# Projection operands kept in DRAM between two token halves, the recurrent unit cut into jobs of its own, the embedding moved to the front

## The chip, the cores and the metric

The kernel runs on one core of one Trainium2 chip. The metric is device time in microseconds. A core has TensorE (PE, matmuls and weight loads), VectorE (DVE), ScalarE (ACT), GpSimd (POOL) and SyncE (SP), which here issues nearly all DMA.

## The reference

One decoder block over 2048 tokens of width 1024, all in float32. Cut to what matters:

```python
xn = rmsnorm(h, pre_gain)
q, k, v, fl, g_attn, x_lru, g_lru = split(xn @ w_in)
o_attn = forgetting_attention(q, k, v, fl + b_f)        # 8 heads of 128, causal, decay bias
y_attn = rmsnorm(o_attn, attn_out_gain) * silu(g_attn)
xc = causal_depthwise_conv(x_lru, conv_w, conv_b)       # width 4
r = sigmoid(xc @ w_r + b_r); i = sigmoid(xc @ w_i + b_i)    # 8 blocks of 128
log_a = -8 * r * softplus(-lam); a = exp(log_a)
u = sqrt(-expm1(2 * log_a)) * (i * xc)
o_lru[t] = a[t] * o_lru[t-1] + u[t]
y_lru = rmsnorm(o_lru, lru_out_gain) * silu(g_lru)
h = h + rmsnorm(concat(y_attn, y_lru) @ w_out, post_gain)
e = rmsnorm(p @ w_ple, ple_gain)
out = h + sigmoid(h @ w_ple_gate + b_ple_gate) * e
```

## The kernel before

Every float32 product is made of three fp32r matmuls (`mm3`): each operand is split into a rounded high part and the remainder (`split`: ACT writes the high part, DVE or POOL the low part).

The input projection is cut into units of two output blocks. A unit multiplies a 2 x 2 arrangement of weight quarters and input quarters in the Strassen-Winograd form: seven products instead of eight. The seven input operands `XH`/`XL` are made once per half of the tokens (1024 of them, p = 0 and 1) by `fill_operand`; the seven weight operands are made for each unit by `Unit.prepare`: sums and differences of the raw quarters `wf` on POOL (`ws`), then the split into `oh` and `ol`, five of each deep (`NOP`). `operand` prepares as far ahead as those buffers allow. Units are of four kinds: v (values and forget logits, the weights moving, 258 columns), k (keys and queries of one head), l (the recurrent input x_lru and its gate g_lru of one block) and g (the attention gate). A k, l or g unit issues 7 x 12 matmuls of 512 columns, a v unit 7 x 4 x 12 of 258 columns. `multiply` issues one product of the seven, `pair` adds the products up; the sum `t5 = t2 + t5` is POOL's, as the split for i = 2 is.

The units run in this order: v 0 of the first half, twenty mixed l, k and g units, v 1 of the first half, v 0 of the second half, sixteen l and k units, v 1, and four g units, marked `light`, for which DVE does what POOL does elsewhere. Two k units are marked `early`: products 0 and 5 of each come before v 0, as soon as the first inputs are there.

An l unit carries the recurrent unit with it (`lru_unit`), on 1024 columns: convolution, gate matmuls (12 of 512 columns), sigmoid, tanh, `Dn = 1/(1 + tanh)` by RECIPROCAL on DVE, square root, scan over time with a carried state, times the gate `G`, store to `yl_d`, and the squares summed in `accl`. Its second part, `gates`, waits in `pending` and is run inside the next unit. Row sums of x for the first norm come from a separate load of x by rows (`row_scales`).

Then comes attention with an order written out by hand, and in the third part the recurrent half of the output mixing with, for each of 16 token blocks, `embed`: 12 matmuls of 512 columns for p @ w_ple, its norm, and a store to `e_d`. The last part mixes the attention half, adds the residual and applies the embedding gate.

Outside the attention part the order on each engine is set by a scheduler that works through the program by priority of program order and its own estimate of times, so an engine's instructions need not stand as the code is written.

## Time and profile before

| what | value |
|---|---|
| three runs, median (lowest to highest) | 2380.26 us (2377.54 to 2383.28) |
| the profiled execution | 2383.02 us |
| its span, first to last instruction | 2381.2 us |
| PE / DVE / POOL / ACT busy share | 92% / 68% / 49% / 44% |
| DMA moved | 276.32 MB |
| granted TensorE clock, mean | 0.969 |

The span is what the trace covers; the run is 1.8 us longer. Shares are means over stages with different limits, so the stages have to be read one by one.

### The profile page before, as it was taken

What the parts mean: (1) busy time and instruction counts of PE and PEld (TensorE: products, weight loads), DVE (VectorE), ACT (ScalarE), POOL (GpSimd) and SP (SyncE); (2) the same over time, 40 slices, a digit from 0 to 9 for tenths busy, and PEclk for the clock granted to TensorE, in tenths of its full rate; (3) what the DMA queues carried; (4) which work ended last, traced back from release to release, by engine and by line L of the source; (5) the groups of instructions that cost most, each with busy time, mean ns of one, the idle gap of its engine ahead of it and who ended that gap; (6) DMA issues with size and microseconds to landing.
All of it is one profiled execution on the core that took longest, in us unless ns stands there. A gap on an engine that the chain in (4) does not pass through costs nothing. (4 is left out here: it accounts for less than half of the span.)

```text
span 2381.2 us, 30652 instructions
## 1 busy us (share of the span) xinstructions
PE 2200.0 (92%) x10753; PEld 1807.6 (76%) x10753; DVE 1612.8 (68%) x2363; ACT 1039.8 (44%) x1786; POOL 1172.8 (49%) x865
## 2 busy tenths in 40 slices
PE   4798899998898999889989999999999999999999
PEld 4676677767786777668768888888878888788887
DVE  5886978788967888887767888887853313333333
ACT  4344444444333433452447676766753423212211
POOL 5766767677666766765312333433453322322221
PEclk9799999999999999999989999999999999999999
DMA  6224232223322222223345444545435535433332
GB/s 217 74 62 126 80 120 82 83 75 110 124 86 74 85 77 69 78 70 101 114 157 133 130 131 139 161 150 144 149 113 164 193 128 186 133 115 111 111 103 83
DMA packets 180922, 276.32 MB, mean 116 GB/s; under 512 B 15392, under 2 KB 84256, under 8 KB 180768
## 3 DMA queue, kind: packets, MB, share of 16 engines
q1 hardware_dynamic: 180624, 274.33, 37.2%
q8 instruction: 84, 1.38, 0.2%
q14 instruction: 70, 0.57, 0.1%
q10 hardware_dynamic: 144, 0.05, 0.0%
HBM read 198.55 MB, written 75.76 MB: 115 GB/s over the span
## 5 line engine op out<-in xcount | busy, mean ns | idle before, releaser
L64 PE MATMUL bank<-XH,oh 128*128 128x512 f32 x1120 | 454.5, 406 | 35.4 <-ACT oh L50 22.4
L66 PE MATMUL bank<-XH,ol 128*128 128x512 f32 x1120 | 450.5, 407 | 35.4 <-DVE ol L56 24.4
L65 PE MATMUL bank<-XL,oh 128*128 128x512 f32 x1120 | 451.0, 403 | 0.0
L66 PEld LDWEIGHTS bank<-XH,ol 128*128 128x128 f32 x1120 | 216.8, 194 | 98.6 <-DVE ol L56 31.8
L64 PEld LDWEIGHTS bank<-XH,oh 128*128 128x128 f32 x1120 | 217.2, 194 | 94.8 <-ACT oh L50 30.4
L65 PEld LDWEIGHTS bank<-XL,oh 128*128 128x128 f32 x1120 | 217.1, 194 | 50.5
L56 DVE TENSOR_TENSOR tl<-tbank,th 128x512 fp32r<-128x512 f32 (+1 forms) x320 | 192.7, 608 | 86.5 <-ACT th L50 82.7
L50 ACT ACTIVATE th<-tbank 128x512 fp32r<-128x512 f32 (+1 forms) x320 | 168.8, 530 | 130.5 <-PE tbank L845 127.4
L50 ACT ACTIVATE oh<-ws 128x512 fp32r<-128x512 f32 (+1 forms) x144 | 90.6, 629 | 267.6 <-POOL ws L215 130.9
L56 POOL TENSOR_TENSOR yo<-yf,yh 128x1024 fp32r<-128x1024 f32 x32 | 76.8, 2401 | 255.2 <-ACT yh L50 255.1
L56 POOL TENSOR_TENSOR ol<-wf,oh 128x512 fp32r<-128x512 f32 (+1 forms) x88 | 129.2, 1471 | 134.7 <-ACT oh L50 120.0
L278 DVE TENSOR_TENSOR c<-bank,c 128x512 f32<-128x512 f32 x208 | 137.9, 680 | 70.9 <-POOL c L292 35.3
L818 ACT ACTIVATE pr<-pr,m 128x128 f32<-128x128 f32 (+15 forms) x128 | 154.0, 1204 | 42.6 <-DVE m L809 41.8
L845 PE MATMUL tbank<-ident,pr 128*128 128x128 f32 x1088 | 172.4, 274 | 0.0
L50 ACT ACTIVATE oh<-wf 128x512 fp32r<-128x512 f32 (+1 forms) x192 | 117.0, 624 | 117.8 <-PE bank L65 57.3
L845 PEld LDWEIGHTS tbank<-ident,pr 128*128 128x128 f32 x1088 | 134.7, 141 | 29.4 <-issue 0.4
L64 PE MATMUL bank<-oh,XH 128*128 128x258 f32 x448 | 133.1, 302 | 24.8 <-ACT XH L50 11.9
L64 PE MATMUL sbank<-kh,qh 128*128 128x512 f32 (+3 forms) x320 | 137.5, 430 | 17.5 <-DVE m L809 17.5
L66 PE MATMUL bank<-oh,XL 128*128 128x258 f32 x448 | 129.7, 298 | 12.3 <-DVE XL L56 12.3
L65 PE MATMUL bank<-ol,XH 128*128 128x258 f32 x448 | 133.3, 300 | 5.7 <-DVE ol L56 3.9
L56 DVE TENSOR_TENSOR ol<-ws,oh 128x512 fp32r<-128x512 f32 (+1 forms) x100 | 101.4, 1015 | 35.0 <-ACT oh L50 34.7
L64 PE MATMUL obank<-th,vh 128*128 128x512 f32 (+1 forms) x320 | 123.5, 386 | 0.8 <-ACT th L50 0.8
(237 smaller groups left out, 5648.5 us busy)
## 6 DMA issues: line engine op xcount, KB each, us to landing
wf<-in_w_p_dram SPq DMA_DIRECT2D x164, 256.0 KB, 2.7
wf<-in_w_v_dram SPq DMA_DIRECT2D x32, 258.0 KB, 3.0
c<-in_x_dram SPq DMA_DIRECT2D x32, 256.0 KB, 4.6
s<-in_xT_dram SPq DMA_DIRECT2D x16, 512.0 KB, 7.8
kT_d<-c SPq DMA_DIRECT2D x32, 256.0 KB, 2.5
qT_d<-c SPq DMA_DIRECT2D x32, 256.0 KB, 2.8
...
yl_d<-G SPq DMA_DIRECT2D x16, 512.0 KB, 2.6
```

Of the source, the lines that this page charges most:

```text
L50: nc.scalar.activation(hi, src, AF.Copy)
L56: eng.tensor_tensor(out=lo, in0=src, in1=f32(hi), op=ALU.subtract)
L64: nc.tensor.matmul(out, lhsT=wh, rhs=xh, start=start, stop=False)
L65: nc.tensor.matmul(out, lhsT=wh, rhs=xl, start=False, stop=False)
L66: nc.tensor.matmul(out, lhsT=wl, rhs=xh, start=False, stop=stop)
L278: nc.vector.tensor_tensor(out=o, in0=x, in1=y, op=ALU.add)
L818: nc.scalar.activation(pr[0][:, :L], pr[0][:, :L], AF.Exp, bias=m2, scale=-1.0, accum_out=u.r4[:, i:i + 1])
L845: nc.tensor.transpose(b[:, i * P:(i + 1) * P], u.P[i][:, sb * P:(sb + 1) * P], ident)
```

## The change

Weight operands: in the first half of the tokens a unit makes each operand as before, in one tile `op` that holds high and low part, and stores it to DRAM (`wo_d`, `vo_d`); in the second half `fetch` loads it, and nothing is made or split. Nine operands can then be held: five `op` and four pairs `wh`, `wl` in the buffers of the raw quarters.

The recurrent unit: an l unit now only stores x_lru to `xr_d` and the gated value of g_lru to `gl_d`. A job (`lru_job`) of 512 columns loads them back, in two steps eight slots apart; a slot is one product (`tick`). Eight of the 32 jobs are planned into the first half, 24 into the second, five slots apart. Instead of the reciprocal a job computes, with `Dn` = 1 + exp(-2z) and two fused steps, one Newton step for 1/(1 + tanh z). R, I, Dn, Q and G have one buffer each.

The embedding is computed first of all, from a pool that is closed before three of the seven input operands are allocated. The column sums of x for the first half's norm come from the already loaded xT (`column_scales`). The two early k units and `light` are gone; the first half runs all l, then all k, then all g units; the second all l, all k, v 1, then g. `t5` and the split for i = 2 are DVE's everywhere.

```diff
+        def fetch(self, i):
+            n = WS if self.kind == "v" else 512
+            for hf in range(self.halves):
+                at_ = state["slot"] % (NOP + NOPB)
...
+                if at_ < NOP:
+                    op = wp.tile([P, 2, WS], F32R, name="op", bufs=NOP)
+                    nc.sync.dma_start(out=f32(op[:, :, :n]), in_=self.stored(i, hf))
+                else:
+                    hi = wp.tile([P, WS], F32R, name="wh", tag="wf", bufs=8)
+                    lo = wp.tile([P, WS], F32R, name="wl", tag="wf", bufs=8)
...
         def prepare(self, i):
+            if self.p:
+                return self.fetch(i)
...
-                split(nc, src, hi[:, :n], lo[:, :n], "act", "pool" if i in (0, 2, 5) and not self.light else "dve")
+                split(nc, src, hi[:, :n], lo[:, :n], "act", "pool" if i in (0, 5) else "dve")
+                nc.sync.dma_start(out=self.stored(i, hf), in_=f32(op[:, :, :n]))
...
-    mids = [("l", 0), ("k", 0), ("g", 0), ("l", 1), ("k", 1), ("l", 2), ("k", 2), ("g", 1), ("l", 3), ("k", 3),
+    mids_A = [("l", n) for n in range(8)] + [("k", n) for n in range(8)] + [("g", n) for n in range(4)]
+    mids_B = [("l", n) for n in range(8)] + [("k", n) for n in range(8)]
...
-        (nc.vector if u.light else nc.gpsimd).tensor_tensor(out=t5, in0=t2, in1=t5, op=ALU.add)
+        add(t5, t2, t5)
...
+    def lru_job(lw, accl, hb, c, t):
+        def first():
...
+            X = lw.tile([P, 515], F32, name="X", bufs=2)
+            nc.sync.dma_start(out=X, in_=xr_d[hb, :, c * 512:c * 512 + 515])
...
+        def second():
...
+                b = sbank()
+                mm3(nc, b, (j.w[0][:, gi], j.w[1][:, gi]), (j.xch, j.xcl), True, True)
+                nc.scalar.activation(dst, b, AF.Sigmoid, bias=vec[:, bias + hb:bias + hb + 1])
+            nc.scalar.activation(Dn, R, AF.Exp, scale=sp4n[:, hb:hb + 1])
             nc.scalar.activation(R, R, AF.Tanh, scale=sp4[:, hb:hb + 1])
-            nc.vector.tensor_scalar(Dn, R, 1.0, None, ALU.add)
-            nc.vector.reciprocal(Dn, Dn)
-            nc.scalar.activation(Q, R, AF.Sqrt, scale=4.0, bias=tiny)
+            nc.scalar.activation(Dn, Dn, AF.Identity, bias=one)
             nc.gpsimd.tensor_tensor(out=I, in0=I, in1=XC, op=ALU.mult)
+            nc.vector.scalar_tensor_tensor(out=Q, in0=R, scalar=1.0, in1=Dn, op0=ALU.add, op1=ALU.mult)
+            nc.vector.scalar_tensor_tensor(out=Dn, in0=Q, scalar=-4.0, in1=Dn, op0=ALU.add, op1=ALU.mult)
+            nc.scalar.activation(Q, R, AF.Sqrt, scale=0.25, bias=tiny)
+            nc.vector.tensor_tensor(out=R, in0=R, in1=Dn, op=ALU.mult)
             nc.vector.tensor_tensor(out=Q, in0=Q, in1=Dn, op=ALU.mult)
+            nc.scalar.activation(Dn, R, AF.Identity, scale=0.5, bias=one)
+            nc.gpsimd.tensor_tensor(out=I, in0=I, in1=Q, op=ALU.mult)
             nc.vector.tensor_tensor_scan(R, Dn, I, carry[:, hb:hb + 1] if c else 0.0, ALU.mult, ALU.add)
+            nc.gpsimd.tensor_tensor(out=G, in0=R, in1=G, op=ALU.mult)
+            nc.sync.dma_start(out=yl_d[hb, :, c * 512:(c + 1) * 512], in_=G)
+                nc.gpsimd.tensor_tensor(out=R, in0=R, in1=R, op=ALU.mult)
+                nc.gpsimd.tensor_tensor(out=acc, in0=acc, in1=R, op=ALU.add)
+        at_slot(t, first)
+        at_slot(t + JLAG, second)
...
+        embed_weights()
+        embeds(1)
         for n in range(2):
-            row_scales(sg, 0, n)
             for kh in range(2):
                 s[n, kh] = stage_tile(sg, 0, n, kh)
+        embeds(5)
+        for n in range(2):
+            column_scales(sg, 0, n, s)
             r = spread_scales(sg, 0, n)
...
+        plan_jobs(lw, accl, 60, 9.5, 8)
...
+        plan_jobs(lw, accl, 1, 5, 8)
+        plan_jobs(lw, accl, 46, 5, 16)
```

Below are three places of the built order. Line numbers are those of the kernel whose order is shown.

First, DVE at the start, before: from the spread norm factor `rx` on, the inputs `s` are scaled and the low parts `XL` of the first two input operands made.

```order
L483 COPY rx<-sbank 128x512
L489 SCALAR_TENSOR_TENSOR s_159<-s_159,vec,rx 128x512 x4
L489 SCALAR_TENSOR_TENSOR s_162<-s_162,vec,rx 128x512 x4
L56 TENSOR_TENSOR XL_109<-s_159,XH_102 128x512 x4
L56 TENSOR_TENSOR XL_114<-s_162,XH_107 128x512 x4
```

DVE at the same place now:

```order
L533 COPY rx<-sbank 128x512
L619 SCALAR_TENSOR_TENSOR eo<-bank,er,pgb 128x512 x2
L518 TENSOR_TENSOR rx<-rx,c 128x512
L539 SCALAR_TENSOR_TENSOR s_186<-s_186,vec,rx 128x512 x4
L539 SCALAR_TENSOR_TENSOR s_189<-s_189,vec,rx 128x512 x4
L619 SCALAR_TENSOR_TENSOR eo<-bank,er,pgb 128x512 x2
L518 TENSOR_TENSOR rx<-rx,c 128x512
L58 TENSOR_TENSOR XL_111<-s_186,XH_110 128x512 x2
L58 TENSOR_TENSOR pl<-pf,ph 128x512
L58 TENSOR_TENSOR XL_111<-s_186,XH_110 128x512 x2
L58 TENSOR_TENSOR XL_113<-s_189,XH_112 128x512 x4
```

The scaled embedding rows `eo`, their splits `pl` and the sums of column squares (`rx<-rx,c`) now stand between the steps that make the input operands; on PE all 192 embedding matmuls stand ahead of the first v unit.

Second, ACT in the second half of the tokens, before: the gates of one recurrent unit (`R`, `I`, tanh into `R`, square root into `X`) among the splits of weight operands (`oh`).

```order
L430 ACTIVATE R<-bank,vec 128x512
L50 ACTIVATE oh<-ws 128x512
L430 ACTIVATE R<-bank,vec 128x512
L430 ACTIVATE I<-bank,vec 128x512
L50 ACTIVATE wgh<-wgf 128x256
L430 ACTIVATE I<-bank,vec 128x512
L431 ACTIVATE R<-R,sp_90 128x1024
L435 ACT_TABLE_LOAD
L435 ACTIVATE X<-R,tiny 128x1024
L50 ACTIVATE oh<-ws 128x512
```

ACT in the second half now, about one job:

```order
L461 ACTIVATE I<-sbank,vec 128x512
L323 ACTIVATE c<-bank 128x512
L440 ACTIVATE XC<-X,vec 128x512
L461 ACTIVATE R<-sbank,vec 128x512
L462 ACT_TABLE_LOAD
L462 ACTIVATE Dn<-R,sp4n 128x512
L52 ACTIVATE xch<-XC 128x512
L463 ACTIVATE R<-R,sp_94 128x512
L464 ACTIVATE Dn<-Dn,one 128x512
L468 ACT_TABLE_LOAD
L468 ACTIVATE Q<-R,tiny 128x512
L414 ACT_TABLE_LOAD
```

The operand splits are gone, the jobs follow each other closely with three table loads each, and the copies that empty PE's banks (`c<-bank`) stand between a job's sigmoids.

Third, SP in the second half, before: raw weights `wf`, results `kT_d` and `qT_d`, gate weights, and the recurrent result `yl_d`.

```order
L190 DMA wf<-in_w_p_dram 128x512 x4
L314 DMA kT_d<-c 128x512
L314 DMA qT_d<-c 128x512
L190 DMA wf<-in_w_p_dram 128x512
L390 DMA wgf<-in_w_gates_dram 128x256
L314 DMA kT_d<-c 128x512
L190 DMA wf<-in_w_p_dram 128x512
L314 DMA qT_d<-c 128x512
L190 DMA wf<-in_w_p_dram 128x512 x2
L445 DMA yl_d<-G 128x1024
```

SP in the second half now:

```order
L477 DMA yl_d<-G 128x512
L341 DMA kT_d<-c 128x512
L431 DMA wgf<-in_w_gates_dram 128x256
L457 DMA G<-gl_d 128x512
L223 DMA op<-wo_d 128x2x512
L341 DMA qT_d<-c 128x512
L223 DMA op<-wo_d 128x2x512 x2
L438 DMA X<-xr_d 128x515
L228 DMA wh<-wo_d 128x512
L229 DMA wl<-wo_d 128x512
L228 DMA wh<-wo_d 128x512
L229 DMA wl<-wo_d 128x512
```

Loads of finished operands stand where raw weights stood, more of them, behind the stores of results and of jobs; the next job's load of `G` stands right behind a job's store.

More of the change, by code (lines that the diff above doesn't have):

```diff
@@ L301, in pair @@
         done(1, 1, t5)
-        for f in pending[:1]:
-            pending.pop(0)()
-        if not u.early:
-            b = multiply(u, 5)
-            o = into(0, t1)
-            add(o, b, t1)
-            done(0, 0, o)
+        add(t1, multiply(u, 5), t1)
+        done(0, 0, t1)
         add(t2, multiply(u, 6), t2)
@@ L449, in gates @@
                 nc.gpsimd.tensor_tensor(out=R, in0=R, in1=R, op=ALU.mult)
[L450 to L454 removed]
+                nc.gpsimd.tensor_tensor(out=acc, in0=acc, in1=R, op=ALU.add)
+            if hb == NH - 1 and half:
+                at_slot(now[0] + 4, lambda: scales_l(p, accl[p]))
+        at_slot(t, first)
+        at_slot(t + JLAG, second)
@@ L565, in hymba_kernel, with plan_jobs @@
-    run_pass(0, units_A[1:-1])
+    jobs = [(h, 2 * p + i) for p in range(2) for h in range(NH) for i in range(2)]
+    def plan_jobs(lw, accl, first, step, n):
+        for i in range(n):
+            h, c = jobs.pop(0)
+            lru_job(lw, accl, h, c, now[0] + int(first + step * i))
+    lam = xp.tile([P, NH], F32, name="lam", bufs=1)
+    lmx = xp.tile([P, NH], F32, name="lmx", bufs=1)
+    z3 = xp.tile([P, NH, 3], F32, name="z3", bufs=1)
+    nc.gpsimd.memset(z3, 0.0)
+    nc.sync.dma_start(out=xr_d[:, :, 0:3].rearrange("h p c -> p h c"), in_=z3)
@@ new lines, in hymba_kernel @@
+    nc.vector.tensor_scalar(lgn, vec[:, LG:LG + NH], -1.0, None, ALU.mult)
+    nc.vector.tensor_copy(lam, vec[:, LAM:LAM + NH])
+    nc.vector.tensor_scalar(lmx, lam, -1.0, 0.0, ALU.mult, ALU.max)
+    for _ in log1p_exp_neg_abs(sp4, lam, xp, NH):
+        pass
+    nc.vector.tensor_tensor(out=sp4, in0=sp4, in1=lmx, op=ALU.add)
+    nc.vector.tensor_scalar(sp4n, sp4, -8.0, None, ALU.mult)
+    nc.vector.tensor_scalar(sp4, sp4, 4.0, None, ALU.mult)
+    with ExitStack() as q:
+        lw = pool_(q, "lw0", side="right")
+        accl = [lw.tile([P, NT], F32, name="accl", bufs=1)]
+        plan_jobs(lw, accl, 60, 9.5, 8)
+        for n in range(2):
+            at_slot(now[0] + 20 + 40 * n, lambda n=n: row_scales(xp, 1, n))
+        for u in units_A[1:-1]:
+            run(u)
+        nc.sync.dma_start(out=acc_d, in_=accl[0])
```

367 lines of the change are left out of this document (193 added, 174 removed).

## The prediction

> **What bounds the kernel now.** I read the page's span, then the busy time by stage, then the groups by line and the waits. The nine stretches are my cut at the stores that end each stage: start with the first v unit; first-half pair units; two v units between the halves; second-half pair units; last v unit; g units; attention; mixing with embedding; output. Columns: PE, weight loads, DVE, ACT, POOL, granted clock, DMA share, GB/s.
>
> ```profile
> span 2381.2 us, 30652 instructions
> ```
>
> ```profile
> 0.00:114.00 114.00, 68.23 (x410) 61.58 (x411) 76.31 (x85) 44.60 (x85) 71.52 (x55) 0.88 0.43 143
> 114.00:581.00 467.00, 426.84 (x1771) 337.09 (x1770) 383.20 (x362) 204.20 (x326) 327.88 (x197) 0.96 0.28 91
> 581.00:694.00 113.00, 95.01 (x678) 90.88 (x677) 96.61 (x115) 38.60 (x63) 83.79 (x56) 0.91 0.38 121
> 694.00:1089.00 395.00, 353.26 (x1457) 276.91 (x1456) 325.88 (x258) 164.64 (x245) 272.10 (x164) 0.96 0.23 74
> 1089.00:1130.00 41.00, 38.27 (x305) 37.90 (x305) 26.71 (x47) 11.08 (x22) 18.53 (x17) 0.97 0.41 122
> 1130.00:1218.00 88.00, 82.29 (x355) 66.30 (x354) 66.15 (x130) 36.31 (x60) 25.82 (x13) 0.96 0.38 116
> 1218.00:1825.00 607.00, 585.52 (x3342) 491.29 (x3343) 447.21 (x1089) 398.17 (x727) 229.13 (x260) 0.99 0.49 140
> 1825.00:2007.00 182.00, 182.00 (x782) 146.92 (x781) 55.98 (x101) 65.94 (x141) 52.52 (x38) 1.00 0.50 167
> 2007.00:2382.00 375.00, 368.54 (x1666) 298.73 (x1664) 134.80 (x183) 76.26 (x120) 91.47 (x68) 1.00 0.38 118
> ```
>
> Matmuls overlap, so a busy PE says little; the rate counts. Undisturbed, a 512-column matmul takes 60/259 = 0.232 us (second row below); a v unit's 336 of 258 columns take its stage's 41 us.
>
> ```profile
> 12.00:24.00 12.00, 3.18 (x8) 2.00 (x8) 7.16 (x15) 6.41 (x17) 1.02 (x1) 1.00 1.03 399
> 1920.00:1980.00 60.00, 60.00 (x259) 48.34 (x258) 10.72 (x22) 15.13 (x32) 11.79 (x8) 1.00 0.38 129
> 1620.00:1680.00 60.00, 58.46 (x339) 49.14 (x338) 49.93 (x123) 41.42 (x75) 26.60 (x32) 1.00 0.64 161
> ```
>
> So each stage has a PE floor, from matmuls counted in the code. First-half pair units: 20 x 84, less 48 done early, plus 96 of gates: 1728 x 0.232 = 401 of 467 us. Two v units: 82 of 113. Second-half pair units and last v: 1440 x 0.232 + 41 = 375 of 436. g units: 336 x 0.232 = 78 of 88. That is 168 us above the floor, with DVE at 82% and POOL at 70% in the pair stages; the longest waits are for operands still being made and split, as this one. Attention and what follows are PE's own.
>
> ```profile
> ACT oh L50 <- POOL ws L215: 130.9, 45, 10.0
> ```
>
> **Embedding.** Its 16 blocks of 12 matmuls leave a stage with PE busy all 182 us: 192 x 0.232 = **-45 us**. PE stays late there: a block's recurrent part needs 48 x 0.232 = 11.1 us, the other engines are at a third. At the front the matmuls meet an idling PE, but DVE's work meets a DVE at 67%.
>
> ```profile
> L1142 DVE SCALAR_TENSOR_TENSOR eo<-ebank,er,pgb 128x512 f32<-128x512 f32 x32 | 22.6, 747 | 12.8 <-POOL er L132 12.8
> L56 DVE TENSOR_TENSOR Wl<-kvf,Wh 128x512 fp32r<-128x512 f32 x8 | 6.7, 843 | 6.0 <-ACT Wh L50 4.6 <-PE ebank L66 1.3
> L466 DVE TENSOR_TENSOR s<-ss 128x4 f32<-128x4 f32 x2 | 0.8, 376 | 14.9 <-ACT c L464 14.9
> L278 DVE TENSOR_TENSOR c<-bank,c 128x512 f32<-128x512 f32 x206 | 136.5, 680 | 67.0 <-POOL c L292 35.3 <-PE bank L66 29.9
> ```
>
> DVE's 76 us gain 32 x 0.75 = 24 of scaling, 12 x 0.84 = 10 of splits, 14 adds of column squares at 0.68 = 10, about 9 of small operations and v work taken from POOL; the two early units' splits and adds, about 6, go. That is 123. PE's floor is 192 x 0.232 + 41 = 86. Bounds: 114 (contention falls and pays for it all) and 161 (all of DVE's present 38 us of idle stays). I take 138, nearer to the busy time: of the idle, 15 us were the wait for the row sums of x (third row), which go, while the first loads, the embedding's 1 MB among them, still have to land. ACT takes on 48 squares of 0.58 (half of L431's 1.16, below) and gives up 16, some 19 us on its 45; POOL takes on 16 powers of a single column; both stay below DVE: **+24 us**.
>
> **First-half pair units.** The 48 early matmuls come back, 96 of gates become 48 (eight jobs): floor 401 as before. What was late eases. DVE did per head, in 1024 columns, these steps:
>
> ```profile
> L432 DVE TENSOR_SCALAR Dn<-R x16: 681/1272/2298, 156.2 to 1068.3; 128x1024 f32<-128x1024 f32 x16
> L433 DVE RECIPROCAL Dn<-Dn x16: 6535/6548/6554, 158.3 to 1069.1; 128x1024 f32<-128x1024 f32 x16
> L437 DVE TENSOR_TENSOR X<-X,Dn x16: 1207/1219/2329, 167.0 to 1077.3; 128x1024 f32<-128x1024 f32 x16
> L439 DVE TENSOR_SCALAR Dn<-Dn x16: 679/1780/1797, 171.0 to 1081.2; 128x1024 f32<-128x1024 f32 x16
> L440 DVE TENSOR_TENSOR_SCAN R<-Dn,I x8: 2274/3268/3283, 173.3 to 568.7; 128x1024 f32<-128x1024 f32 x8
> ```
>
> ```profile
> L430 ACT ACTIVATE R<-bank,vec x32: 670/686/695, 152.4 to 1063.4; 128x512 f32<-128x512 f32 x32
> L431 ACT ACTIVATE R<-R,sp x16: 1143/1156/1167, 155.0 to 1064.5; 128x1024 f32<-128x1024 f32 x16
> ...
> L435 ACT ACTIVATE X<-R,tiny x16: 1149/1154/1158, 158.5 to 1068.0; 128x1024 f32<-128x1024 f32 x16
> L443 DVE SCALAR_TENSOR_TENSOR G<-R,vec,G x16: 1267/1648/2548, 179.9 to 1088.0; 128x1024 f32<-128x1024 f32 x16
> L449 POOL TENSOR_TENSOR R<-R x14: 1892/1895/2338, 248.8 to 1089.8; 128x1024 f32<-128x1024 f32 x14
> L450 POOL TENSOR_TENSOR accl<-accl,R x14: 2336/2399/3252, 251.2 to 1093.9; 128x1024 f32<-128x1024 f32 x14
> ```
>
> With both multiplies that is 17 us a head, 136 for eight. A job of 512 columns needs two fused steps (half of 1.65), two multiplies (half of 1.22) and the scan (half of 3.27): 4.5, 36 for eight. Half the convolution goes too (24 steps of 0.8). Twenty adds (0.68) and twenty splits (0.84) come over from POOL. DVE: 383 - 100 - 20 + 31 = 294, 70% of 421.
>
> New there is DMA: each unit now stores 3.67 MB of operands besides 1.05 loaded and 1.05 of results. Twenty units, eight jobs and x make 126 MB, 299 GB/s over 421 us. By share, the rows bound what DMA can carry: 399/1.03 = 387 GB/s at the start, 91/0.28 = 325 in this stage, 161/0.64 = 252 in attention. At 325, the like traffic, 126 MB take 388 us, under the floor but by 13 us only. Each issue costs SP 0.33 us (first row), and a store lands some 2.6 us later (second):
>
> ```profile
> L314 SPq DMA_DIRECT2D kT_d<-c x32: 319/326/383, 40.8 to 1088.1; - x32
> ```
>
> ```profile
> yl_d<-G SPq DMA_DIRECT2D x16, 512.0 KB, 2.6
> ```
>
> The program has 1369 of them instead of 953: 137 us more of SP, spread over some 1180, hidden. Behind a store that waits for its split stand the next raw loads, but operands are made up to five ahead, 14 us. Idle kept: between 0 and today's 66 us; I take 20, since both loads fall and DMA rises: 421, **-46 us**.
>
> **The v units between.** 25 MB in 82 us of floor is 78 us at 325 GB/s. DVE's filling of the operands for the second half stays; the second unit's splits (ten of 0.84 us or more) go, 97 to 88. Between 82 and 113 I take 100: **-13 us**.
>
> **Second half.** Loaded operands free ACT, DVE and POOL. Nine are held, 25 us ahead; on SP they stand behind the jobs' stores and the next job's G load, which waits for that store to land, 2.6 us of SP each time against those 25. X and G come back from memory units after they were stored, so that trip is off the path. 24 jobs instead of 16 make the floor (1344 + 144) x 0.232 + 41 = 386. Eight us of other stalls remain (3.67 MB a unit in 105 MB total: 325 us, hidden). What is late next is the job itself. Its buffer R is single: written by the sigmoid, last read by POOL's add; the next sigmoid waits for that, and behind it on ACT stand the copies that empty PE's banks. The same chain in one unit before:
>
> ```profile
> 826.46 0.67 ACT L430 ACTIVATE R<-bank,vec 128x512 f32<-128x512 f32 x1
> ...
> 828.47 1.15 ACT L431 ACTIVATE R<-R,sp 128x1024 f32<-128x1024 f32 x1
> 829.64 1.28 ACT L435 ACT_TABLE_LOAD   x1
> 830.94 1.15 ACT L435 ACTIVATE X<-R,tiny 128x1024 f32<-128x1024 f32 x1
> ```
>
> ```profile
> 830.31 2.84 POOL L436 TENSOR_TENSOR I<-I,XC 128x1024 f32<-128x1024 f32 x1
> ...
> 856.31 2.34 POOL L450 TENSOR_TENSOR accl<-accl,R 128x1024 f32<-128x1024 f32 x1
> ```
>
> It lasted 32.2 us, for 25 us of work by the rows above: 1.29 times. The new chain at 512: sigmoid 0.69, table load 1.28, exp, tanh and identity 0.58 each, one foreign pass 0.6, two fused steps 0.82 each, square root 0.58, multiply 0.61, POOL multiply 1.42, scan 1.63, POOL multiply 1.42, square 0.95, add 1.2: 13.8. Times 1.29 is 17.8, and the next job's I·XC, 1.42, stands ahead of the square in about a third: L = 18.3. Bounds: 13.8, and 17.8 + 1.4 + a second load 1.3 + an l unit's load and sigmoid 1.9 = 22.4.
>
> In PE's new order the gates stand 60 matmuls apart, 66 x 0.232 = 15.3 us, with one gap of 30.6: 367 us from the first job to the last. PE can be one period ahead. So PE loses 23 L - 367 - 15 where that is positive (L over 16.6): 39 at 18.3, nothing at 13.8, 133 at 22.4. Stage: 386 + 8 + 39 = 433, **-3 us**.
>
> The load behind tanh began 0.02 us after it and the root 0.02 us after the load: 1.30 in all. The Trainium skill (ScalarE: Activation LUTs, What ACT_TABLE_LOAD costs) adds about 1.38 us of drain to each switch. By that L is 19.7 and the loss 71, and the sum would be 32 us later. The trace shows no such drain here, so 1.28 stands.
>
> **The rest.** g units: 88 to 86, their idle being mostly the handover to attention: **-2 us**. Attention and output issue what they did, behind PE: 0, unless the handover shifts.
>
> **Sum.** +24 - 46 - 13 - 3 - 2 - 45 = -85: span 2296. The profiled run took 2383.0, 1.8 over its span, and 2.8 over the median of the runs: 2295 us.
>
> **Rivals.**
> All stages near PE's floor (0.20): the slack of DVE and POOL speaks for it, the chain's 1.29 and the thin DMA cover against. Start +10, then 409, 90, 394, 82, -45: -164, 2216.
> The job chain eats it all (0.12): at L = 22.0 the loss is 124, 85 more, 2380; above, slower. For it: table loads rise from 36 to 108 in the order. Against: after the l units, ACT's foreign work ends.
> DMA is the bound (0.09), the other side: loads and stores together reach less than 252 GB/s. First half 126/0.252 = 500 (+79 on forecast), v units 100: -6, no change; at 235, 536, 108 and 449: +54, 2435. Against it stand 325 and 387; no row shows both directions full.
> A second table load on each chain, the square root's, where nothing covers it (0.04): L = 19.6, loss 69, 2326. For it speaks that both loads stand in the order; against it that the two fused steps of DVE, 1.65 us, run meanwhile. The drain that the Trainium skill (ScalarE: Activation LUTs, What ACT_TABLE_LOAD costs) states comes to nearly the same.
> The start keeps all of DVE's idle: 161 us there, 2319, inside the forecast's range.
>
> **How the numbers follow.** Forecast, 2255 to 2335 by the bounds of L and the start: 0.50, with the second-load case inside it beside. Floor 0.20, chain 0.12, DMA 0.09, the remaining 0.05 between 2335 and 2375. Leaving out DMA, half the chain case and a little of the floor case: 2212 to 2372. A measurement tells 0.2%, 5 us. Faster: 0.50 + 0.04 + 0.20 + 0.05 + 0.05 of the chain case = 0.84; same 0.04; slower 0.12.
>
> **What would show it.** Right: mixing blocks of 11 us instead of 14 behind attention; a first stage near 138 us with DVE at 85% or more; first-half pair units near 421 us with DMA at 0.8 to 0.9; second-half jobs some 17 us apart or more, with ACT's gate sigmoid waiting for POOL's add. The prediction is wrong where PE waits for operand loads, where the first-half pair units stay at 467 us with DMA at 1.0, or where the jobs keep to 15.3 us and PE does not wait at all.

## The result and the profile after

The changed kernel takes 2341.52 us (median of 4 runs, 2337.64 to 2341.79) against 2381.59 us for the kernel before in the same comparison: ratio 0.983, 95% interval 0.9813 to 0.9847, 40 us faster. The forecast was 2295 us. The direction was right, but half of the gain was missing, and the time lies above the forecast's range of 2255 to 2335 us. The profiled execution:

```profile
span 2340.0 us, 31563 instructions
```

The busy times by stage follow, in the nine stretches and with the columns that the prediction used (length, PE, weight loads, DVE, ACT, POOL, granted clock, DMA share, GB/s), cut at the same places of the work.

```profile
0.00:146.00 146.00, 105.45 (x577) 90.95 (x578) 112.65 (x205) 64.23 (x138) 66.87 (x63) 0.89 0.59 213
146.00:580.00 434.00, 417.51 (x1782) 335.32 (x1781) 281.65 (x347) 214.88 (x350) 247.63 (x173) 0.98 0.83 292
580.00:675.00 95.00, 81.63 (x631) 80.04 (x630) 74.50 (x106) 24.34 (x39) 35.68 (x21) 0.95 0.81 273
675.00:1077.00 402.00, 372.37 (x1621) 300.97 (x1620) 235.58 (x314) 240.89 (x315) 169.48 (x133) 0.97 0.77 242
1077.00:1117.00 40.00, 32.01 (x210) 29.21 (x209) 23.64 (x42) 20.54 (x29) 18.93 (x18) 0.92 0.66 212
1117.00:1222.00 105.00, 85.77 (x363) 68.79 (x361) 56.73 (x106) 38.89 (x55) 38.72 (x23) 0.90 0.56 190
1222.00:1829.00 607.00, 585.33 (x3342) 492.34 (x3343) 447.93 (x1092) 399.26 (x728) 228.02 (x260) 0.99 0.45 140
1829.00:1966.00 137.00, 137.00 (x600) 112.40 (x599) 15.94 (x17) 39.05 (x57) 43.16 (x22) 1.00 0.42 133
1966.00:2340.00 374.00, 365.15 (x1657) 298.82 (x1655) 133.03 (x183) 76.31 (x120) 90.98 (x68) 0.99 0.37 118
```

| stage, us | before | forecast change | after | change |
|---|---|---|---|---|
| start, first v unit | 114 | +24 | 146 | +32 |
| first-half pair units | 467 | -46 | 434 | -33 |
| v units between | 113 | -13 | 95 | -18 |
| second-half pair units, last v unit | 436 | -3 | 442 | +6 |
| g units | 88 | -2 | 105 | +17 |
| attention | 607 | 0 | 607 | 0 |
| mixing and output | 557 | -45 | 511 | -46 |

DVE fell from 325.88 us in 395 to 235.58 in 402 in the second-half pair units, and nothing became faster there: that engine was relieved and something else took its place as the limit. The largest miss is the g units, for which the forecast had almost no change.

**One job in the second half.** The chain that the prediction named is there. First ACT, from one gate sigmoid `R` to the next (start, length, engine, line, operation; in brackets the idle time before it and what ended it):

```profile
891.84 0.69 ACT L461 ACTIVATE R<-sbank,vec 128x512 f32<-128x512 f32 x1 [0.34 <-POOL accl L480]
892.54 1.28 ACT L462 ACT_TABLE_LOAD   x1
893.84 0.72 ACT L462 ACTIVATE Dn<-R,sp4n 128x512 f32<-128x512 f32 x1
894.47 0.80 ACT L440 ACTIVATE XC<-X,vec 128x512 f32<-128x512 f32 x1
895.17 0.71 ACT L463 ACTIVATE R<-R,sp 128x512 f32<-128x512 f32 x1
895.79 0.71 ACT L464 ACTIVATE Dn<-Dn,one 128x512 f32<-128x512 f32 x1
...
899.39 1.28 ACT L468 ACT_TABLE_LOAD   x1 [0.61 <-DVE Dn L467]
900.68 0.72 ACT L468 ACTIVATE Q<-R,tiny 128x512 f32<-128x512 f32 x1
...
910.23 0.69 ACT L461 ACTIVATE R<-sbank,vec 128x512 f32<-128x512 f32 x1 [2.41 <-POOL accl L483]
```

Then DVE and POOL in the same job:

```profile
896.76 0.69 DVE L466 SCALAR_TENSOR_TENSOR Q<-R,Dn 128x512 f32<-128x512 f32 x1
...
898.63 0.68 DVE L467 SCALAR_TENSOR_TENSOR Dn<-Q,Dn 128x512 f32<-128x512 f32 x1
...
901.71 0.68 DVE L469 TENSOR_TENSOR R<-R,Dn 128x512 f32<-128x512 f32 x1
902.31 0.69 DVE L470 TENSOR_TENSOR Q<-Q,Dn 128x512 f32<-128x512 f32 x1
...
904.47 1.28 DVE L473 TENSOR_TENSOR_SCAN R<-Dn,carry,I 128x512 f32<-128x512 f32 x1 [0.28 <-POOL I L472]
```

```profile
903.14 1.30 POOL L472 TENSOR_TENSOR I<-I,Q 128x512 f32<-128x512 f32 x1 [2.68 <-DVE Q L470]
905.84 1.30 POOL L476 TENSOR_TENSOR G<-R,G 128x512 f32<-128x512 f32 x1 [1.40 <-DVE R L473]
907.21 1.04 POOL L482 TENSOR_TENSOR R<-R 128x512 f32<-128x512 f32 x1
908.21 0.74 POOL L58 TENSOR_TENSOR wgl<-wgf,wgh 128x256 fp32r<-128x256 f32 x1
908.90 1.29 POOL L483 TENSOR_TENSOR accl<-accl,R 128x512 f32<-128x512 f32 x1
```

Read them as one list and there is hardly a hole in it: from 891.84 to 910.23 one link follows the other across the three engines, with a few foreign instructions in between, and the second sigmoid waits for the last add on the single buffer `R`. Over the whole half the group of that sigmoid gives the mean: 24 of them, the first at 699.0, the last at 1134.9.

```profile
L461 ACT ACTIVATE R<-sbank,vec x24: 687/688/697, 699.0 to 1134.9; 128x512 f32<-128x512 f32 x24
```

(1134.9 - 699.0) / 23 = 18.95 us a job; the forecast had 18.3. PE feels it through the gates: these are all its waits in the second-half pair units (673 to 1052 us), first for the bank that the sigmoid empties, then for the sums of squares that POOL adds up:

```profile
PE sbank L66 <- ACT R L461: 18.1, 8, 3.7
PE sbank L149 <- POOL accl L483: 7.9, 2, 7.1
```

**The g units.** These are PE's waits from 1117 to 1222:

```profile
PE sbank L731 <- issue: 11.9, 1, 11.9
PE bank L66 <- ACT c L322: 4.8, 1, 4.8
PE sbank L149 <- POOL accl L483: 2.4, 1, 2.4
```

L731 are the matmuls of the bias rows. They need the prefix sum of log1p (`zz`, made by DVE's scan at L723), which starts from the forget logits `zf`. These were complete at 1117 us, but their transpose (L708) stands on PE right behind the transposes of the row sums (L149), and those wait for the last add of the last job. Then DVE waits 18.9 us for POOL's eight powers, and L731 begins when the scan is done, though the view names no releaser for it (`issue`):

```profile
1153.21 0.66 PE L149 MATMUL sbank<-ident,accl 128*128 128x128 f32 x4 [2.45 <-POOL accl L483]
1153.71 0.27 PE L708 MATMUL sbank<-ident,zf 128*128 128x128 f32 x1
...
1188.75 0.42 DVE L723 TENSOR_TENSOR_SCAN zz<-za,lsn 128x128 f32<-128x128 f32 x1
```

POOL after, then POOL before, from the last add of the last job:

```profile
1151.89 1.26 POOL L483 TENSOR_TENSOR accl<-accl,R 128x512 f32<-128x512 f32 x1
...
1158.85 22.95 POOL L126 TENSOR_TENSOR l1y<-two,za 128x16 f32<-128x16 f32 x8 [0.57 <-DVE za L122]
```

```profile
1093.95 2.34 POOL L450 TENSOR_TENSOR accl<-accl,R 128x1024 f32<-128x1024 f32 x1
...
1137.96 23.76 POOL L116 TENSOR_TENSOR l1y<-two,za 128x16 f32<-128x16 f32 x8 [7.73 <-DVE za L112]
```

Before, the last recurrent unit was done at 1096.3 and the powers waited for the forget logits of the last v unit; now the last job ends at 1153.2 and everything behind it, up to attention, follows. The first attention matmul began 118 us after the end of the recurrent part before, and 66.6 us after it now.

### The profile page after: what moved, and what is told of

Read it like the earlier page. It is cut to its first block, busy times and chain, and to the rows that moved or that the text cites. A ratio compares the mean times of both kernels' runs of the same rounds, so it can differ in the third digit from the quotient of the medians.

```text
span 2340.0 us, 31563 instructions
## 1 busy us (share of the span) xinstructions
PE 2182.2 (93%) x10769; PEld 1808.8 (77%) x10769; DVE 1381.7 (59%) x2409; ACT 1118.4 (48%) x1826; POOL 939.5 (40%) x777
## 4 chain that ended last, share of the span: by engine, by line
PE 51%; DVE 5%; ACT 5%; POOL 5%; issue 4%; DMA 4%; SPq 0%; POOLq 0%; DVEq 0%; ACTq 0%
PE bank L66 11%; PE bank L68 10%; PE bank L67 10%; PE tbank L978 4%; PE sbank L66 3%; PE sbank L68 2%; PE sbank L67 2%; PE obank L67 2%; PE obank L68 2%; PE obank L66 2%; POOL accl L483 1%; DVE R L473 1%; ACT pr L951 1%; POOL I L465 1%; POOL R L482 1%
## 5 line engine op out<-in xcount | busy, mean ns | idle before, releaser
L68 PE MATMUL bank<-XH,op 128*128 128x512 f32 x860 | 344.4, 400 | 10.8 <-DVE op L58 8.2
L66 PE MATMUL bank<-XH,op 128*128 128x512 f32 x860 | 344.7, 401 | 3.2 <-ACT op L52 3.2
L67 PE MATMUL bank<-XL,op 128*128 128x512 f32 x860 | 343.3, 399 | 0.0
L68 PEld LDWEIGHTS bank<-XH,op 128*128 128x128 f32 x860 | 164.2, 191 | 53.5 <-DVE op L58 13.9
L66 PEld LDWEIGHTS bank<-XH,op 128*128 128x128 f32 x860 | 164.7, 192 | 43.3 <-ACT op L52 4.7
L67 PEld LDWEIGHTS bank<-XL,op 128*128 128x128 f32 x860 | 164.2, 191 | 38.8
L443 DVE SCALAR_TENSOR_TENSOR XC<-X,vec,XC 128x512 f32<-128x512 f32 x96 | 93.6, 977 | 69.6 <-ACT XC L440 68.7
L66 PE MATMUL bank<-op,XH 128*128 128x258 f32 x384 | 113.0, 296 | 9.0 <-DVE o L316 4.3
L67 PE MATMUL obank<-tl,vh 128*128 128x512 f32 (+1 forms) x320 | 118.6, 371 | 1.2 <-DVE tl L58 1.2
L68 PE MATMUL obank<-th,vl 128*128 128x512 f32 (+1 forms) x320 | 117.6, 367 | 0.0
L68 PE MATMUL sbank<-kh,ql 128*128 128x512 f32 (+3 forms) x320 | 116.6, 364 | 0.0
L67 PE MATMUL sbank<-kl,qh 128*128 128x512 f32 (+3 forms) x320 | 116.5, 364 | 0.0
```

The costliest lines, as they stand in the source:

```text
L66: nc.tensor.matmul(out, lhsT=wh, rhs=xh, start=start, stop=False)
L67: nc.tensor.matmul(out, lhsT=wh, rhs=xl, start=False, stop=False)
L68: nc.tensor.matmul(out, lhsT=wl, rhs=xh, start=False, stop=stop)
L443: nc.vector.scalar_tensor_tensor(out=XC, in0=X[:, i:i + 512], scalar=vec[:, CW + 8 * i + hb:CW + 8 * i + hb + 1], in1=XC, op0=ALU.mult, op ...
```

## The experiments

The kernels ran in four groups, each beside the kernel before; ratios are to it, and its median lay between 2383.0 and 2387.7 us in them. The first two rows are of the comparison above. Spans are cut at PE's own matmuls (the first matmul of each kind of stage; the g units begin at the last matmul of the last v unit, and "rest" at the first score matmul of attention), so they differ by some us from the table above. L is the mean distance of the gate sigmoids of all second-half jobs, "tail" the time from the last job's last add to the first attention matmul. With twelve jobs in the first half L is set by the wider plan and left out.

| kernel | median us | ratio (95%) | start | first half | v units | second half | last v | g | rest | L | tail |
|---|---|---|---|---|---|---|---|---|---|---|---|
| before | 2381.59 | 1 | 112 | 461 | 114 | 393 | 49 | 85 | 1167 | - | 118 |
| changed | 2341.52 | 0.9830 (0.9813-0.9847) | 142 | 425 | 106 | 379 | 58 | 110 | 1120 | 18.95 | 66.6 |
| A scan in Q | 2275.68 | 0.9543 (0.9527-0.9559) | 142 | 427 | 108 | 348 | 45 | 92 | 1113 | 16.2 | 64.9 |
| B bias later | 2338.76 | 0.9809 (0.9788-0.9830) | 142 | 425 | 106 | 379 | 58 | 110 | 1115 | 18.95 | 67.1 |
| A+B | 2274.44 | 0.9535 (0.9519-0.9551) | 142 | 424 | 109 | 348 | 45 | 92 | 1113 | 16.2 | 65.0 |
| C embedding at the end | 2343.07 | 0.9825 (0.9806-0.9843) | 105 | 422 | 106 | 380 | 56 | 113 | 1157 | 18.95 | 69.3 |
| D operands made anew | 2487.69 | 1.0440 (1.0417-1.0462) | 141 | 430 | 118 | 419 | 58 | 201 | 1117 | 24.6 | 65.4 |
| A+D | 2453.77 | 1.0292 (1.0273-1.0312) | 141 | 429 | 117 | 449 | 68 | 131 | 1118 | 22.5 | 68.1 |
| E reciprocal | 2283.98 | 0.9589 (0.9566-0.9611) | 141 | 422 | 101 | 349 | 48 | 109 | 1112 | 17.25 | 67.6 |
| A+E | 2258.95 | 0.9479 (0.9458-0.9500) | 141 | 419 | 106 | 341 | 45 | 89 | 1118 | 15.7 | 68.7 |
| F product in XC | 2314.71 | 0.9712 (0.9697-0.9726) | 142 | 431 | 106 | 364 | 58 | 99 | 1115 | 18.0 | 65.5 |
| A+E, 4 jobs first | 2251.12 | 0.9446 (0.9432-0.9460) | 143 | 397 | 103 | 357 | 46 | 89 | 1115 | 14.1 | 67.2 |
| A+E, 4 jobs first, 4.4 | 2257.64 | 0.9472 (0.9457-0.9487) | 142 | 397 | 103 | 354 | 51 | 92 | 1117 | 14.3 | 68.8 |
| A+E, embedding split | 2260.84 | 0.9490 (0.9475-0.9504) | 122 | 418 | 106 | 341 | 45 | 89 | 1140 | 15.7 | 69.1 |
| A+E, third `eo` | 2260.65 | 0.9482 (0.9466-0.9498) | 144 | 421 | 106 | 341 | 45 | 89 | 1115 | 15.7 | 68.8 |
| 12 jobs first | 2310.20 | 0.9697 (0.9675-0.9720) | 141 | 459 | 114 | 345 | 43 | 90 | 1112 | - | 70.2 |
| 4 jobs first | 2383.78 | 1.0001 (0.9991-1.0010) | 141 | 400 | 102 | 398 | 56 | 169 | 1115 | 19.1 | 66.3 |

My theory was that the chain of jobs through the single buffers, 18.95 us each, sets the second half and through its end the g units. The rivals: fetched operands, the DMA traffic or an engine's load.

**A: the scan writes Q.** `R` is then read for the last time by the identity of L471, and what follows no longer holds the next sigmoid.

```diff
-nc.vector.tensor_tensor_scan(R, Dn, I, ...)
+nc.vector.tensor_tensor_scan(Q, Dn, I, ...)
 ...            # carry, G, squares and accl read Q instead of R
```

> Edit: in a job the scan writes its result into Q instead of R, and the carry, the G product and the squares read it there; nothing else. Theory (the chain of jobs through the single buffer R sets the second half): R is read for the last time by the identity of L471, some 11 us after the sigmoid and no longer at the end of accl, some 18.5 us after it. Then the next chain is bounded by Q (first written 4.9 us after the sigmoid, 891.84 to 896.76, and read last by accl at 910.2), so a job takes about 13.5 to 14 us instead of 18.9. The 23 jobs of the second half need some 320 us instead of 436, less than the PE floor of 394, so that stretch falls from 442 to 400-410, the jobs end before the g units and these fall from 105 to about 90: 2341.5 - 35 - 15 = about 2290, between 2275 and 2305. Rival (the wait is carried by the fetched operands, SP's queue or POOL's load and not by R's buffer): the R starts move but PE still waits for xch and op; 2330 to 2345.

Measured 2275.68 us, 66 us under the changed kernel, at the good end of what the chain foretold. L fell to 16.2 us and not to 13.5 or 14: the forecast's plan puts 367 us between the first and the last job, 16.0 a job, so what is left is the pace at which PE brings the jobs. The stage of the second-half pair units, here 676 to 1024.5, has PE busy nearly throughout at clock 1.00; in the changed kernel the same matmuls take 673 to 1052:

```profile
676.00:1024.50 348.50, 343.14 (x1477) 277.30 (x1476) 227.26 (x307) 230.52 (x302) 164.98 (x129) 1.00 0.85 269
```

```profile
673.00:1052.00 379.00, 352.97 (x1475) 282.02 (x1474) 224.10 (x298) 226.74 (x295) 157.09 (x124) 0.97 0.78 245
```

Of the 30 us, 21 are idle time of PE (26.0 us against 5.4) and 10 are busy time at the lower granted clock, 0.97; why the clock was lower is not shown. DVE, ACT and POOL do the same work in both, and the distance of the jobs differs. So none of these engines, nor the traffic (269 GB/s in the shorter stretch against 245), was the limit. The edit also lets the scheduler place other instructions differently, so the 66 us are those of the edit with its new order. The same holds for every edit below that touches a job.

**B: the bias scan's call behind the second g unit.**

```diff
-        cm = bias_scan()
         g_unit(units_B[-3])
-        bias_rows(*cm)
+        bias_rows(*bias_scan())
```

> Edit: bias_scan is called after the second g unit instead of before it; the jobs are untouched. Theory (the g units' 17 us extra is the eight powers of log1p, 23 us on POOL, for which VectorE waits in order 18.9 us while it should evict the second g unit): the second g unit runs under the powers, PE's gap of 12.3 us goes, and the jobs' chain stays as it is; 2341.5 - 8 to 12 = 2329 to 2334. Rival (the g units are late because the jobs' tail itself holds PE's banks): same, 2339 to 2344. Second rival: the log1p then ends later and attention waits for the bias instead: same.

Measured 2338.76 us, no difference. The edit is empty: the order of instructions on each engine is the same as in the changed kernel, since the scheduler and not the order of these calls places them. So it tests nothing, and is a second measurement of the changed kernel (0.9809 and 0.9830); differences of this size between kernels say nothing here.

**A+B.** Empty beside A for the same reason, and a second measurement of it.

> Edit: both of the two before. Theory: with the short chain the jobs end well before the g units and the powers begin early, so that the second edit has nothing left to gain: within 5 us of the scan-in-Q kernel, 2275 to 2305. If the two were independent causes, it is the sum of both differences, some 10 us under the scan-in-Q kernel.

2274.44 and 2275.68 us.

**C: the embedding back in the mixing stage.**

```diff
-        embed_weights()
-        embeds(1)     # and the other blocks at the start
 ...
+            embed(tb)     # in the mixing stage, once per block of rows
```

> Edit: the embedding's 16 blocks are put back into the mixing stage, as in the kernel before; stores and jobs stay as in the changed kernel. Theory (the embedding costs 32 us at the start and saves 45 us in mixing, apart from the rest): the start goes back to 114 us, mixing to its old span: 2341.5 - 32 + 45 = 2354, between 2345 and 2362. Rival (the later start is owed to the other edits, and the embedding is nearly hidden where it is): the start stays at 135 or more and the time is 2375 to 2390. Other rival (the embedding hidden at the end beside DVE and POOL that the jobs left): 2315 to 2335, and the move was a loss.

Measured 2343.07 us: the same as the changed kernel, though 2354 was expected. The start is 37 us shorter and what follows attention 40 us longer. In its first 105 us DVE is busy 86.68 us, instead of 112.65 in 146. The embedding's work is hidden in neither place; moving it was worth nothing within the measurement.

**D: the operands made anew in the second half, nothing stored.**

```diff
-            if self.p:
-                return self.fetch(i)
-                nc.sync.dma_start(out=self.stored(i, hf), in_=f32(op[:, :, :n]))
```

> Edit: no weight operand is stored to DRAM; the second half makes them anew from the weights, as in the kernel before. Jobs and embedding as in the changed kernel. Theory (the jobs' chain sets the second half, and the operand work on VectorE and GpSimd lies in the same in-order queues as the chain's links): the first half loses the stores and is at most 10 us shorter, the chain gets longer by 1 to 2 us a job for 23 jobs, +25 to +45 us: 2350 to 2380. Rival (stores and fetches cost as much as the recomputation, the chain is not touched): 2332 to 2347. Rival (the DMA traffic of the stores holds the first half): 2310 to 2330.

Measured 2487.69 us, far above every expectation: 146 us over the changed kernel. The first half did not become shorter without the stores (430 against 425), so their traffic cost nothing there. The jobs got 24.6 us apart, not 20 to 21: (24.6 - 18.95) x 23 = 130 of the 146 us. The operand work stands on ACT, DVE and POOL between a job's links, and each job pays 5.65 us for it.

**A+D.**

> Edit: the same with the scan in Q, so that a job's chain no longer sets the second half. Theory (once the chain is short, VectorE would be busy some 320 of 350 us in the second half, as before the change, and no longer keeps up with PE's banks and the jobs): 2290 to 2310, which is 15 to 35 us over the scan-in-Q kernel with stored operands. Rival (hidden under PE): 2270 to 2280, and the stores brought nothing.

2453.77 us: 178 us over A, where 15 to 35 were expected. The engines' busy time would have fitted; the jobs, still 22.5 us apart, and the operands now wait for each other.

**E: the reciprocal put back in the jobs.**

```diff
-            nc.scalar.activation(Dn, R, AF.Exp, scale=sp4n[:, hb:hb + 1])
             nc.scalar.activation(R, R, AF.Tanh, scale=sp4[:, hb:hb + 1])
-            nc.scalar.activation(Dn, Dn, AF.Identity, bias=one)
-            nc.vector.scalar_tensor_tensor(out=Q, in0=R, scalar=1.0, in1=Dn, ...)
-            nc.vector.scalar_tensor_tensor(out=Dn, in0=Q, scalar=-4.0, in1=Dn, ...)
+            nc.vector.tensor_scalar(Dn, R, 1.0, None, ALU.add)
+            nc.vector.reciprocal(Dn, Dn)
 ...
-            nc.vector.tensor_tensor(out=R, in0=R, in1=Dn, op=ALU.mult)
-            nc.scalar.activation(Dn, R, AF.Identity, scale=0.5, bias=one)
+            nc.vector.tensor_scalar(Dn, Dn, 2.0, -1.0, ALU.mult, ALU.add)
```

> Edit: the reciprocal is put back in the jobs (exponential, identity and two products removed; one add, one reciprocal of 128x512, some 3.3 us by half of the 6546 ns that 128x1024 took before, and one small affine step put in); separate jobs as in the changed kernel. Theory (chain): its links change by -0.7 -0.7 -1.4 -0.7 +0.4 +3.3 +0.4 = about +0.6 us, so 23 jobs make +14 us: 2345 to 2365. Rival (the reciprocal on VectorE holds evictions, as it did before the change): over 2365. Rival (no difference): 2338 to 2345.

The sign was wrong: 2283.98 us, 57 us faster than the changed kernel. L fell to 17.25, and the table loads of the whole kernel from 108 to 68. On ACT, tanh now follows the sigmoid at once, and the square root follows with its load; nothing waits for DVE:

```profile
897.96 0.69 ACT L461 ACTIVATE R<-sbank,vec 128x512 f32<-128x512 f32 x1 [3.43 <-POOL accl L480]
898.68 0.72 ACT L462 ACTIVATE R<-R,sp 128x512 f32<-128x512 f32 x1
...
900.13 1.28 ACT L466 ACT_TABLE_LOAD   x1
901.43 0.72 ACT L466 ACTIVATE Q<-R,tiny 128x512 f32<-128x512 f32 x1
```

and the reciprocal, on DVE, runs beside that load:

```profile
900.82 3.35 DVE L464 RECIPROCAL Dn<-Dn 128x512 f32<-128x512 f32 x1
```

My list for the expectation had counted instructions and left out two things that the rows of the changed kernel show: the exponential has a table load of its own behind the sigmoid (892.54), and the square root's load begins only when the second fused product is done (899.39, idle until `DVE Dn L467`).

**A+E.**

> Edit: the same with the scan in Q. Theory: the chain has 1 to 2 us of room against the 15.3 us at which the jobs are planned, so nothing or a few us: 2273 to 2285. Rival (VectorE's 3.3 us of reciprocal holds PE's banks): 2290 to 2310.

2258.95 us, 82 us under the changed kernel and better than expected. Beside A the reciprocal brings 17 us instead of 57: the two gains overlap, as they shorten the same chain.

**F: the first fused product into XC.** This keeps the instructions of a job and takes away what makes the square root wait.

```diff
-nc.vector.scalar_tensor_tensor(out=Q, in0=R, scalar=1.0, in1=Dn, ...)
-nc.vector.scalar_tensor_tensor(out=Dn, in0=Q, scalar=-4.0, in1=Dn, ...)
+nc.vector.scalar_tensor_tensor(out=XC, in0=R, scalar=1.0, in1=Dn, ...)
+nc.vector.scalar_tensor_tensor(out=Dn, in0=XC, scalar=-4.0, in1=Dn, ...)
```

> Edit: the changed kernel, but the first fused product of a job is written into XC, which is free by then, instead of Q; the square root, whose result goes to Q, then waits for the tanh alone and no longer for VectorE's two fused products. The number of table loads stays. Theory (putting the reciprocal back helped because the square root and its table load stood behind the two products, 34 us of idle in 32 jobs, in the chain): a job shortens by about 2 us, to 16.7 to 17.4 us from 18.95, and as 17.25 us gave 57 us with the reciprocal: 2280 to 2300. Rival (the reciprocal's gain was the exponential's table load of 1.28 us, identity and four products less, whatever the square root waits for): 2325 to 2342.

2314.71 us: between the two, 27 of the 57 us. The groups of the square root's table loads (count, busy us, mean ns, idle before them), of the changed kernel and then of this one:

```profile
L468 ACT ACT_TABLE_LOAD x32 | 41.1, 1283 | 34.3 <-DVE Dn L467 34.2
```

```profile
L468 ACT ACT_TABLE_LOAD x32 | 41.1, 1283 | 0.6
```

As many loads before the square roots, the wait gone, L 17.99: by this kernel, whose order is new too (102 table loads in all instead of 108), about half of the cost of the form without reciprocals is that the temporary was put into the square root's output buffer. The other half is the rest of that form: the exponential with its load, the identity, the additional products. These were not taken apart further.

**A+E with four jobs in the first half.** In this spacing the last row sums of the first half are read only after a later job has begun to overwrite them, so that part of the computation differs; the amount of work is the same.

```diff
-        plan_jobs(lw, accl, 60, 9.5, 8)
+        plan_jobs(lw, accl, 60, 19, 4)
 ...
-        plan_jobs(lw, accl, 1, 5, 8)
-        plan_jobs(lw, accl, 46, 5, 16)
+        plan_jobs(lw, accl, 1, 4.4, 12)
+        plan_jobs(lw, accl, 53, 4.5, 16)
```

> Edit: on the kernel with scan in Q and reciprocal (2259 us), four instead of eight jobs run in the first half (19 units of the calendar apart instead of 9.5), twelve and sixteen in the second, 4.4 and 4.5 apart instead of 5. Theory (the first half's idle above its floor is owed to the jobs there, which begin at 335 us; without jobs PE had no gaps): the first half falls from 419 to 408-414 us, the second half pays 4 x 6 matmuls = 6 us of floor and the chain at 13.7 us each just keeps up: 2250 to 2262. Rival (the traffic of the stores, 0.85 of the DMA engines, holds the first half): first half 419, second half longer by 6 to 20: 2265 to 2280.

2251.12 us, inside the range: the first half fell by 22 us to 397, more than expected, the second grew by 16. The traffic of the stores is not what holds the first half.

**The same with 55 and 4.4 in the last line**, which restores the order of the row sums:

> Edit: scan in Q, reciprocal, and four jobs in the first half as before, the last sixteen from 55 on and 4.4 apart, so that the row sums of the first half are read ahead of the next write. The best that these parts promise: 2245 to 2258, as the kernel with 4.5 between them (2251).

2257.64 us, at the edge of the range. It and A+E (2258.95) are the fastest complete kernels here and cannot be told apart.

**A+E with the embedding split**, `embeds(1)` and `embeds(5)` at the start, blocks from the seventh on in the mixing stage:

> Edit: on the kernel with scan in Q and reciprocal (2259 us), six of the embedding's 16 blocks stay at the start, ten go back to the mixing stage. With all 16 at the end the start was 37 us shorter and the mixing stage 40 us longer. Theory (the first blocks run while the first loads land and cost less than the later ones, which stand in VectorE's way): start 112 to 120 instead of 141, mixing 25 longer (10/16 of 40): 2255 to 2262. Rival (the start's cost is the same for each block): start 119, the same total within 5 us. Rival (all six hidden): start 105, 2248.

2260.84 us, the same as A+E: start -19, end +22. The theory and its first rival both had this total; a start of 122 us fits the rival better. Every block costs about the same in both places.

**A+E with a third `eo`** and its store on the other queue:

```diff
-eo = te.tile([P, D], F32, name="eo")
+eo = te.tile([P, D], F32, name="eo", bufs=3)
-nc.sync.dma_start(out=e_d[ts, :], in_=eo)
+nc.scalar.dma_start(out=e_d[ts, :], in_=eo)
```

> Edit: on the kernel with scan in Q and reciprocal (2259 us), the embedding's output buffer has three instances instead of two and its store is issued from ScalarE's queue instead of SyncE's. Theory (ScalarE waited 33 us for that store to free the buffer, SyncE 52 us for the scaling, and other loads stood behind it): the start falls by 8 to 15 us, 2243 to 2252. Rival (the start is set by VectorE's normalisation standing between the embedding's steps, and the buffer's wait is only its shadow): within 4 us of 2259.

2260.65 us, no gain: the long waits on that buffer were a shadow. The first v unit began 18 us earlier (81.8 us instead of 99.5), but the pair units behind it began no earlier (143.9 instead of 141.2).

**Twelve jobs in the first half**, `plan_jobs(lw, accl, 60, 6, 12)`, then `(1, 5, 4)` and `(22, 6.5, 16)`, otherwise the changed kernel:

> Edit: the changed kernel with twelve jobs in the first half, six units of the calendar apart, and four and sixteen in the second, the sixteen from 22 on and 6.5 apart. Theory (a job costs some 5.5 us in the first half, where its chain is not the limit, and a chain's length of 18.95 us in the second; attention can begin no earlier than 66 us after the last job, as in seven kernels so far, 65 to 69): first half 425 + 22 = 447; the second half's 20 jobs keep to the calendar, pair units some 345 instead of 379, last v unit 45 instead of 58, g units 90 instead of 110: 2341.5 + 22 - 34 - 13 - 20 = 2296, between 2280 and 2312. Rival (a job costs the same wherever it runs): 2335 to 2350.

2310.20 us, 31 us faster, inside the expectation. The second half is nearly where A has it (345, 43, 90) with the long chain in place, as these jobs are planned further apart than the chain is long (19.2 us from one to the next); four more jobs cost the first half 34 us.

**Four jobs in the first half of the changed kernel**, the calendar of the 55 and 4.4 version:

> Edit: the changed kernel with four jobs in the first half and 28 in the second, on the same calendar as the one before; scan in R, no reciprocal. Theory (28 jobs of 18.95 us in a row, the first at 677, the last ends at 1207, attention begins 66 us later, at 1273 instead of 1220): 2395, between 2375 and 2405, although the first half is 22 us shorter. Rival (the gain of fewer jobs in the first half is free, as in the short-chain kernel, 8 us): 2330 to 2342.

2383.78 us, 42 us slower than the changed kernel and back at the time before, though its first half is 25 us shorter. PE's longest waits from 1098 to 1270 of this kernel show where it went; POOL's last add ends at 1200.8.

```profile
PE sbank L731 <- DVE zz L723: 33.1, 1, 33.1
PE sbank L149 <- POOL accl L483: 26.6, 2, 14.4
```

Attention was expected at 1273 and began at 1267. Four jobs instead of eight in the first half bring 1 to 8 us with the short chain and cost 42 us with the long one.

## Why the prediction was half right

The misses by stage, start first, are 8 + 13 - 5 + 9 + 19 - 1 = 43 us of the 85 that were forecast.

**Mixing, -45: right.** -46 came.

**Start, +24: came as +32.** The failed step is the idle time of DVE, of which I kept 15 us. 33 us stayed (146 less 112.65), while the busy time was below my 123. DVE works in order, and one block of the input's scaling stands between two small steps of the embedding:

```profile
80.42 0.16 DVE L614 TENSOR_TENSOR es<-ess 128x1 f32<-128x1 f32 x1 [0.65 <-ACT eo L612]
80.50 11.64 DVE L539 SCALAR_TENSOR_TENSOR s<-s,vec,rx 128x512 f32<-128x512 f32 x8
92.06 0.14 DVE L141 TENSOR_SCALAR rs<-es 128x1 f32<-128x1 f32 x1
```

PE's longest wait of the stage, 13.5 us for a bank, ended with the embedding's scaling (`eo`) that came behind them. But this wait is not what set the stage: with the third `eo` PE's waits for `eo` fell from 21.0 to 10.4 us, and the stage was no shorter. There DVE was busy 55.5 of the 57 us from that block of scaling to the end of the stage. So what remains is how late the block comes: 21 of the 33 us of DVE's idle time lie ahead of it, in the first 80 us of the changed kernel. That the order of the embedding's steps is what delays it was not tested by itself. The start is 37 us longer than without the embedding there (C), and that costs nearly all of the 40 us gained at the end.

**First half, -46: came as -33.** The failed step is "idle kept: I take 20"; 33 us stayed over the floor of 401. They are mostly the eight jobs. I had costed them by their matmuls and DVE's time. Four fewer save 22 us with A+E (419 to 397) and 25 in the changed kernel; four more cost 34. Of this the floor explains 4 x 6 x 0.232 = 5.6 us. In the changed kernel PE waits 13.9 us in this stage, 11.4 of them for weight operands that ACT and DVE still split; with four jobs it waits 1.9. From the first job on the granted clock is 0.96 instead of 0.99, too; why is not shown. The DMA traffic, which I had as the nearest limit, is not it: without the stores the stretch was 430, and before the first job PE has no gap although the DMA share is higher there (0.94) than behind it (0.76):

```profile
142.00:335.00 193.00, 193.00 (x832) 155.99 (x832) 109.82 (x146) 77.26 (x148) 90.20 (x67) 1.00 0.94 328
```

**v units, -13: -18 came**, on the good side.

**Second half, -3: +6 came, and g units, -2: +17 came.** The mechanism was the forecast's: a job's single buffer, released by POOL's add, and PE late by it. Two steps failed. The smaller is the size of L. 18.95 instead of 18.3 makes 23 x 0.65 = 15 us. My list of links gave 13.8 us with one table load and 0.6 for a foreign pass. The rows above, from start to start, give 18.39: 2.65 of foreign work (the next job's convolution on ACT and on DVE, a bank's addition, a split of gate weights) and 15.74 of the job's own, 2.5 more than my list. Half of this is the second load, 1.29: I had it as a rival at 0.04, with 19.6 us, because two fused steps of DVE would run meanwhile. They do not, since the square root waits for them, so that rival's mechanism is there. The factor 1.29 that I took from the old unit made up for most of what the list lacked: that the total came near was luck.

The larger step is the end of that chain. I priced the lag inside the second-half stage alone and let the g units keep their 86 us. But the lag does not end at a stage's border: the last job ended 57 us later than before (1153.2 against 1096.3), and behind it stand on one string the row sums, POOL's 23 us of powers, the bias rows and attention. Before, this string had 118 us and hid behind PE's work; in all sixteen kernels with jobs it takes 65 to 70 us, whatever the rest: 34 to 38 from the row sums to L731 and 31 to 33 from there to attention (before: 87 and 31). Where the jobs end late against PE's other work, PE reaches L731 first and waits: 11.9 us in the changed kernel, 17.8 in E, 33.1 in the last experiment. In five kernels with enough room, A+E among them, it does not wait there; in those the 65 to 70 us are PE's own work in the order that the scheduler gave it. The 17 us of the g units follow from there: 11.9 and 2.4 of the waits shown are new, the third was 4.5 before, and PE's busy time grew by 3.5 us (82.29 to 85.77) at a granted clock of 0.90 instead of 0.96.

**The parts are not independent.** Taken out of the changed kernel one at a time, the stored operands are worth 146 us, the embedding's place nothing, and the form without reciprocals costs 57. So the 40 us are a large gain, mostly spent on a longer chain; with a shorter chain (A+E) the same change takes 123 us off the kernel before. Cutting the recurrent unit into jobs was not taken out by itself. I had summed the parts by stage, and took the freed engines' time as the measure; what counted was the length of one job, 15.3 us of PE's work against 18.95 of links.

On the table load: a load took 1283 ns and the next activation began 0.01 us after it (899.39 + 1.28, then 900.68). The Trainium skill ("ScalarE: Activation LUTs", "What ACT_TABLE_LOAD costs") adds a drain of about 1.38 us to each switch. No run here shows one: with no wait in the way, the product-in-XC kernel's loads had 0.6 us of idle ahead of 32 of them together. The measurement decides, and the 1.28 us of the forecast stood.

## What to carry to other kernels

When an engine is relieved, write down the longest loop through a single buffer, link by link across the engines, with the other work that stands between the links in order, and compare its period with the work that PE has for each turn. Then follow the last turn on to the next stage: a lag is not paid where it arises but where the last thing that hangs on it is needed. An instruction that is cheaper for one engine can be dearer for the chain: here 3.35 us of reciprocal beside a table load cost the chain less than an exponential with a load of its own and two products ahead of the square root's load.
